# Pairing the 64x64 products of a triangular inverse across four heads, with a new order of the whole program

## The chip, the cores and the metric

The program runs on one core of one Trainium2 chip. The metric is the device time of one execution in microseconds, taken as the median of several runs; lower is better. Five engines work side by side and meet through semaphores: TensorE (PE, with its weight loads shown apart as PEld), VectorE (DVE), ScalarE (ACT), GpSimd (POOL) and SyncE (SP), which here only issues transfers.

## The reference, cut to what matters

One decoder layer on a 1024 x 1024 input: an input projection, two groups of heads (a gated linear recurrence and a gated delta rule), an output projection, and a squared-ReLU MLP. The change lies in the delta rule. Each of its four heads cuts the sequence into chunks and solves a unit lower triangular system in each:

```
Lmat = jnp.where(strict, jnp.einsum('bhnid,bhnjd->bhnij', k_beta, k) * decay, 0.0)
tmat = Lmat + jnp.eye(C, dtype=jnp.float32)
u = lax.linalg.triangular_solve(tmat, v_beta, left_side=True, lower=True, unit_diagonal=True)
w = lax.linalg.triangular_solve(tmat, k_beta * jnp.exp(g)[..., None], ...)
```

The kernel takes chunks of 128 rows, so that there are 8 chunks a head and 32 triangular matrices of 128 x 128. It inverts them once and multiplies by the inverse.

## The kernel before, in words

**Stages.** The start brings in the input `x`, normalizes it, computes a scale `A1` from `w_mod` (`scale0`, `scale1`) and multiplies with the weights of the key projection as they land (`wk0` to `wk3`, each 512 KB; `wk0` comes in two halves). Then come the projections of keys, z, queries, values and the recurrent group, the delta rule among them (`key`, `inverse`, `query`, `value`, `chain`), the output projection, and the MLP: an up stage and a down stage, each of them a seven-product scheme of the Strassen kind. Large products split an operand into a high and a low part (`xh` by an ACT cast, `xl` by a DVE subtraction) and take three matmuls (`mm3`).

**The down stage.** It computes seven products, numbered `at` = 1, 2, 6, 5, 7, 3, 4 (line 1648), each over eight steps `d`. A step needs a left operand `L{d}_{at}` and a right one `R{d}_{at}`, each loaded from DRAM as 512 KB into one slot and split into two more slots (`L..h`, `L..l`); for `at` 5 and 7 POOL first subtracts a second loaded block from the right operand. 24 matmuls use a pair. The last products go to the banks `dn13` and `dn4b`, half a bank each, and DVE, ACT and POOL turn them into the last rows of the output (`final_parts`, line 1561).

**The inverse.** `inverse` (line 956) first inverts all 32 x 32 diagonal blocks, then fills in the off-diagonal parts: `it` and `iy` with 32 x 32 products for two groups of two heads, then `iw` and `iz` with 64 x 64 products for each head. Per head, `iw(h)` is one product a chunk from the lower to the upper half of the partitions, `after_iw` (ACT, line 1020) scales it into `AW`, and `iz(h)` takes that back from the upper to the lower half; `after_iz` (DVE) copies it into `LT`, which `chain` reads. The two kinds of product use different quarters of the PE array. `mms` (line 442) records a list of matmuls as one entry; every head's `iw` or `iz` is two entries of four products (`q0` = 0, 4). `mixed` (line 1026) puts two lists into one entry, in turn. Before the change, heads are handled in pairs (0, 1) and (2, 3): `iw` of the first alone, `iw` of the second mixed with `iz` of the first, `iz` of the second alone (lines 1040 to 1050).

**The order.** Nothing runs in the order of the code. A `Recorder` (line 240) takes every operation with its dependences; `emit` (line 306) issues them by a written-out list `ORDER`, unpacked from the literal `_ORDER` (line 115). Each engine, and each queue of transfers, works through its own part of that list strictly in order, and waits for what an entry depends on. `SLOTS` (line 217) says which of the 46 and 6 slots of 512 KB in the on-chip memory, or of the 8 PSUM banks, a tile gets; a tile can be written only when the last reader of the slot's tile before is done. Most operations pass through one helper, so the profile puts them on L319, those of `mms` on L445; tiles are known by name.

Of the kernel before, what the change touches and what calls it, by code (L numbers as in the profile page):

```python
# [106 lines left out]
def dram_box(ap):  # L107
# [12 lines left out]
    'I^tDH6_Iq&R(DZ0x`y4mou80mv`ebeR_RE3uZ+yY-Dv+uXD*5MxiQ9Bvz1mzb$m;cXu2#hcAO}zH4n7v(fxE2{iCepjl|MYxe2SO!MgvqO*VRl24K&<D1pvl'  # L120
    'EuLLj5&pt7f+nA%Z$!s!<6BF9o@$I_SbZ4@*n5{{t<*-Zpq1lE$uJm!FL^nG`aOX!nGDIx7tDi!SZ*fsGQN`wn6I7P<>yk53e#Nl&u_=_Y>#vkgP#m}Q-;wT'
    'tmtw3WVs1YBi@T$bfGUHx!1_8HVJ!5lije6!}wkRe+yG3*$1t(gr%I72C&&yauls+OG{Y*ZLXl!@*C{4C9Q>)?w4(}QB<@0qyX%>Jr$O<*j)ozO<Adtd<D5Q'
    'hLt42Dn`Jjs$w-)rMql_b{^mzrYk)_6LD`KX3v2q@8J6T;12F5ea#qe6xLe+vbh2|K5xA!mYpoeKwcMd_p-ekkL#TDn(t?W;79S0PJj;5RPGjRMn6h#*h7l+'
    '#_IFaD%mb-TiLMx47nk{N;7x{W1b1nZvncO{*?N7eulD39QQCEQ!2e~CXw1-8qG3?vG)ob1A9rLhh!ywrcgTlW`c4L$H`pjhQ14=E#06^<{)O8>-`!GU`;n9'
    'JFF>aXNt#+yCjeIQt*3Rb&_ke1T9soKf}K3&=$FA+hv0$u2Mm%$}yPX8hpI0nNM43G%Rd9?=?5!V{ENQe{Q00$P(P=4;dii=s`}G{aF7I!*l_wJZO?lX^ywP'
    'x7+NZ!Mxoh$Xx1(H7u0+yvsa5Ur>r1G1a*-tv08;4Z*EIfmnak3P76B44ZJ(nR;0)DnkeGEsM9<EHFVz<_^KZJX`jf80@Sd=b$&ZzxkGyQWeT)ddp<056c2l'
    'V!Z(w&r4(>tklpf>||rq#Pn=(otjZjpiVBVI+kAJQ6_;}+gTgR<iN;`R?w^>c2Sy44@-cz(a2y{=$`3A`We6HNlPvbTMfY9bC8(zR1afAl5`*Bo0ap>VRMG^'
# [1596 lines left out]
```

## Time and profile before

| | us |
|---|---|
| median of 3 runs | 1123.45 |
| lowest and highest run | 1123.28, 1124.21 |
| span of the profiled execution | 1121.3 |
| PE busy in the span | 1111.5 |
| DVE, ACT, POOL busy in the span | 795.0, 622.0, 254.0 |

The profile shows one execution, from its first to its last instruction; what the runs add around the span is 2.15 us. No time of its own is given for the profiled execution beside the span, so a change of the span is added to the median. Matmuls overlap: the record of a 512-column matmul lasts about 395 ns, while the next one starts after about 232 ns, so what a matmul costs is read from the starts of two neighbours.

### The profile page before, as it was taken

What the parts mean: (1) busy time and instruction counts of PE and PEld (TensorE: products, weight loads), DVE (VectorE), ACT (ScalarE), POOL (GpSimd) and SP (SyncE); (2) the same over time, 40 slices, a digit from 0 to 9 for tenths busy, and PEclk for the clock granted to TensorE, in tenths of its full rate; (3) what the DMA queues carried; (4) which work ended last, traced back from release to release, by engine and by line L of the source; (5) the groups of instructions that cost most, each with busy time, mean ns of one, the idle gap of its engine ahead of it and who ended that gap; (6) DMA issues with size and microseconds to landing.
All of it is one profiled execution on the core that took longest, in us unless ns stands there. A gap on an engine that the chain in (4) does not pass through costs nothing.

```text
span 1121.3 us, 16537 instructions
## 1 busy us (share of the span) xinstructions
PE 1111.5 (99%) x6282; PEld 934.3 (83%) x6282; DVE 795.0 (71%) x1122; ACT 622.0 (55%) x967; POOL 254.0 (23%) x159
## 2 busy tenths in 40 slices
PE   9999999999999999999999999999999999999997
PEld 8889889999988877888888888788888888888886
DVE  4859886877878796888675767768664583874573
ACT  6549644466488973786555545556555333453352
POOL 1000100101011442100113123132400366903030
PEclk9999999999999999999999999999999999999999
DMA  9808716567632354321777586778999757954511
GB/s 348 257 20 293 252 38 184 162 195 244 209 96 95 114 206 128 135 85 58 262 239 285 189 277 234 257 243 310 401 397 396 257 183 256 335 173 179 206 75 75
DMA packets 127688, 234.00 MB, mean 209 GB/s; under 512 B 10933, under 2 KB 51450, under 8 KB 127610
## 3 DMA queue, kind: packets, MB, share of 16 engines
q1 hardware_dynamic: 127370, 232.73, 59.8%
q8 instruction: 49, 0.80, 0.3%
q10 hardware_dynamic: 240, 0.23, 0.1%
q14 instruction: 29, 0.24, 0.1%
HBM read 174.18 MB, written 58.74 MB: 208 GB/s over the span
## 4 chain that ended last, share of the span: by engine, by line
PE 93%; ACT 2%; DVE 1%; DMA 1%; issue 1%; SPq 1%; POOL 0%; POOLq 0%; ACTq 0%; DVEq 0%
PE dn L319 27%; PE upx L319 16%; PE upz L319 8%; PE q_p L319 4%; PE k_p L319 4%; PE v_p L319 4%; PE wg L319 4%; PE upy L319 4%; PE ly_p L319 4%; PE lx_p L319 4%; PE wl L319 3%; PE z_p L319 3%; PE ch L319 2%; PE cho L319 1%; DMA wk<-in_w_in_dram 1%
## 5 line engine op out<-in xcount | busy, mean ns | idle before, releaser
L319 PE MATMUL upx<-h2h,U 128*128 128x512 f32 x512 | 167.9, 395 | 0.0
L319 PEld LDWEIGHTS upx<-h2h,U 128*128 128x128 f32 x512 | 96.2, 188 | 22.5
L319 ACT ACTIVATE act<-act 128x512 f32<-128x512 f32 x112 | 70.8, 632 | 58.6 <-DVE act L319 56.5
L319 PE MATMUL upx<-h2l,U 128*128 128x512 f32 x256 | 101.1, 395 | 0.0
L319 POOL TENSOR_TENSOR wd<-wd,wd 128x512 f32<-128x512 f32 x32 | 46.4, 1452 | 236.2 <-DMA wd<-in_w_down_dram 143.5
L319 DVE TENSOR_TENSOR U<-wu,U 128x512 fp32r<-128x512 f32 x112 | 84.4, 776 | 20.7 <-ACT U L319 19.7
L319 PE MATMUL upz<-h2h,U 128*128 128x512 f32 x256 | 85.0, 394 | 0.0
L319 ACT CAST U<-wu 128x512 fp32r<-128x512 f32 x112 | 65.4, 617 | 19.9 <-DVE wu L319 18.2
L319 PEld LDWEIGHTS upx<-h2l,U 128*128 128x128 f32 x256 | 48.1, 188 | 11.8 <-issue 0.4
L319 PEld LDWEIGHTS upz<-h2h,U 128*128 128x128 f32 x256 | 48.1, 188 | 11.1
L319 ACT COPY ek<-upx 128x512 f32<-128x512 f32 x48 | 28.0, 583 | 51.3 <-PE upx L319 50.8
L319 PE MATMUL upz<-h2l,U 128*128 128x512 f32 x128 | 50.3, 393 | 0.0
L319 DVE TENSOR_TENSOR act<-upz,ek 128x512 f32<-128x512 f32 x32 | 22.1, 690 | 36.7 <-ACT ek L319 17.9
L319 POOL TENSOR_TENSOR R<-R,R_5o 128x1024 f32<-128x1024 f32 x8 | 24.5, 3077 | 80.6 <-DMA L<-aod 69.9
L319 PE MATMUL upy<-h2h,U 128*128 128x512 f32 x128 | 42.7, 395 | 0.0
L319 DVE TENSOR_TENSOR wu<-wu,wu 128x512 f32<-128x512 f32 x48 | 36.0, 760 | 2.1 <-DMA wu<-in_w_up_dram 1.9
L319 ACT ACT_TABLE_LOAD x24 | 30.8, 1283 | 2.5 <-issue 2.1
L319 POOL TENSOR_TENSOR ssq<-ssq,mhalf 128x1 f32<-128x1 f32 x16 | 12.8, 805 | 81.1 <-DVE ssq L319 81.0
L319 PE MATMUL q_p<-hh,q_wh 128*128 128x256 f32 (+2 forms) x96 | 30.1, 339 | 0.0
L319 PE MATMUL v_p<-hh,v_wh 128*128 128x256 f32 (+2 forms) x96 | 29.8, 340 | 0.0
L319 PE MATMUL q_p<-hl,q_wh 128*128 128x512 f32 (+2 forms) x96 | 29.7, 336 | 0.0
L319 PE MATMUL lx_p<-hh,lx_wh 128*128 128x256 f32 (+2 forms) x96 | 29.6, 333 | 0.0
(576 smaller groups left out, 3468.4 us busy)
## 6 DMA issues: line engine op xcount, KB each, us to landing
L<-aod SPq DMA_DIRECT2D x56, 512.0 KB, 5.1
R<-in_w_down_dram SPq DMA_DIRECT2D x40, 512.0 KB, 7.2
wu<-in_w_up_dram SPq DMA_DIRECT2D x32, 512.0 KB, 4.5
aod<-as SPq DMA_DIRECT2D x64, 256.0 KB, 5.6
wd<-in_w_down_dram SPq DMA_DIRECT2D x32, 512.0 KB, 5.2
aod<-act SPq DMA_DIRECT2D x48, 256.0 KB, 2.7
x<-in_x_dram SPq DMA_DIRECT2D x16, 512.0 KB, 3.6
sc_w<-in_w_mod_dram SPq DMA_DIRECT2D x16, 512.0 KB, 7.9
```

The costliest lines, as they stand in the source:

```text
L319: op.fn(*[res(v) for v in op.a], **{n: res(v) for n, v in op.k.items()})
```

## The change

`inverse` now steps over the heads: `iw(0)` alone, then `iw(h)` mixed with `iz(h - 1)` for h = 1, 2, 3, then `iz(3)` alone. The products are the same 64; they stand in 10 entries instead of 12. `iw(2)` and `iz(1)`, which stood alone, now share two entries.

```
-        for g in (0, 2):
+        for h in range(NH + 1):
             for q0 in (0, 4):
-                mms(iw(g, q0))
-            after_iw(g)
-            for q0 in (0, 4):
-                mms(mixed(iw(g + 1, q0), iz(g, q0)))
-            after_iz(g)
-            after_iw(g + 1)
-            for q0 in (0, 4):
-                mms(iz(g + 1, q0))
-            after_iz(g + 1)
+                mms(mixed(iw(h, q0), iz(h - 1, q0)) if 0 < h < NH else iz(h - 1, q0) if h else iw(h, q0))
+            if h:
+                after_iz(h - 1)
+            if h < NH:
+                after_iw(h)
```

Both literals are replaced as well, and that reaches the whole program. Unpacked (base85, zlib, running sums), the old list has 8199 entries and the new one 8197. Read engine by engine, with the recorded operations beside them:

| | old list | new list |
|---|---|---|
| PE entries | 5469 | 5467 |
| PE entries that keep their order (longest common run in order) | | 2493 |
| DVE, ACT, SP entries that keep their order | | 797 of 1122, 668 of 914, 356 of 543 |
| slots with the same number | | 90 of 1572 |
| stretches of `iw`, `iz` and second `iy` on PE, with full-size matmuls between stretches | iw0; iw1+iz0; iz1 then iy1; iw2; iw3+iz2; iz3 | iw0 then iy1 then iw1+iz0; iw2+iz1; iw3+iz2; iz3 |
| full-size PE entries from iw2 to the next stretch, and from there to iz3 | 7, 7 | 4, 4 |
| stretches of the start's small products (`sc1_r`) | 2 | 4 |
| before the first matmul that needs the second half of `wk0`: transposes of `x`, key matmuls | 17, 7 | 20, 10 |
| first 13 transfers on SP | | the same |
| PE in the down stage: share of entries that follow their neighbour in the code | 0.95 | 0.01 |
| down stage: fewest matmuls from the last read of a slot by PE to the first matmul on an operand loaded into it | 145 | 28, 36, 42, 43, 47 |
| down stage: the same for an operand part split into a slot | 50 | 8, 8, 9, 9, 12 |
| entries on `dn4b` after the last one on `dn13`, at the end | 24 | 16 |

The 28 belongs to `R5_6` (`at` 6, loaded from a stored sum of `w_down` blocks). The four tightest split parts are `R4_6l`, `R6_2l`, `L0_5l` and `R3_4l`, all made by a DVE subtraction. In the new list of DVE, at the end, the order is: the scaling of `dn13` (`t`), its addition to `xb`, the last pass for `fin6`, that for `fin7`, and then the scaling of `dn4b`.

More of the change, by code (lines that the diff above doesn't have):

```diff
@@ L120 @@
[L120 to L127, printed above, removed]
@@ new lines @@
+    'f;IH>s2V{kOQ}<NqPeDXTRH?~3vF3s+R<wJLwhboEWwXAb`(awdE?UOv?)<Zc<wr!)HHP3M&k*MF`Bq!6#^rJlreJ;yuqTA$aFvRj+WT5T(1!c}?YVg8TNymE}sdE^6'
+    'qUQX%`y-iZ}PPwiTj;53S9LpzdWtD!e)#MtVChC1sME2=AO_kzm=R~BAoYr)5DYSb{)5|ULmb|KO>lJ-kCdgpDphNhd82vuAFf&MyRPWX1G+C}_C(hZX%jvb3mglnzq'
+    'j&P5R*`3AyspqPSoRMcFOBqJ`dO+E$pWp-cU!as=dWbOrDeU|K?{FqR9=#oXyXCdphd8>ldFupGktxoz2sXhDrS*U`k?%zx6<nE(nM7TXf8RW**Nz_ox$9)%boHo7C5'
+    'VU<gzAmwbJra=3zfn^2<>@r!8f+Hj$E=-NpU$Ar?r)Zl$EKWYsyL-KehRSb51#%ZdE0(JwSbI>-=xnO45!y9@MulAdeHVp_xh?mM507Ek(W8Q!^UJ}!WNu4@*s^{kB0'
@@ new lines @@
+    '0rIAv)pz*xrgo7T`Y$<wy{~9)#-9#Pf6X|ZG-9L+bhkbw1^GTv&gp#32tFcmQB}Pz(IbpMt88bE)uSs@heRJpy<dK2>^Z?(5%-7B&y442GiI8Ht1`Q&ob|KtX9wBAHA'
+    'VUEb!|mYMFaMx=qPzk%gI>q(pW#2J2h2H^ZjN0p0PCs<&&hWEY<sEkbdV^Fu%2WUbksIIig!NKj*au^~bcUj*%+ZV;881$`iCuOLBp>wOU4JgX;)>y}(R<z>0}-nDI1'
+    'X)JJJ&yVjA<^bz^f8`9q+j{eXF%;qd-C(=%D{?y-yl@(Z_dU#zZ2XrBpyGrlMTwla;@8}Wfg55J><xy%^p4BAzNbC7`lCoSeyeD$x3U-{$yF_pwk;nLyB(vpyy>wHg*'
+    'VdlIM@Np`8a<qv0P?=od?4?8SJ!uyVVV%4`v{giL{ycKjf|upGrz>RD!IabwrtjYx*yMftZihfwv)%{b7&aTnn*T1E7`z$DgP`uXz3>T#T;2r6qSuQ=@mPy7vvVkQ%B'
@@ new lines @@
+    'cEBdJxf>{fli?ewFGf(Pj95>_-WC@bx;a2BcQF6zIurB0R>IvxM+)soEhcdg7{Mrjphv>b*g8R9eg*DS|s0k>R7$Pa!Ap12IU8p`LAgl{IvGg$R2Sn;wH!#*V?Me0Vf'
+    '%W%I)pV4vB4C`FhOj5xu_L-%jo9Qi*X89+aVhKZk=D>Ryq_O+P&-Gq1>Nt1Am*Lpv|Kiv+eDf5qTmL!|l^1oe`xZOz@NM{<!}aus7+X5tP4+W&qATdf^8K^=F|m_Cge'
+    '>A%J>m_P&|xl%zbMJ_6Qj;4h5ZtD9weX9iT>ZNobHxe^=FyuKbH3Tsa)}fi&RaCOws53IBB5cBfVo&iRU$b0v1h_bwuK2jdAs2cg`=CvA(@)=X1$kSJWGpY~~4!Vwqc'
+    '|ANu`Zs)Qtov2e-gVqd`b0uO6lg8WIYQQZVq4{25SFjXtT0e|XMea}yjh49fi-WQdUKBN0a+V~XNDH-$(?L4g$B%dyDRq*y{O@<3DXog^?Y`jko&mRH>PTujqF`9LfA'
@@ new lines @@
+    'KxX)ammT+3He@M(d8}+ky6<ob6fR<UegM)(6@A_bb)W?#^Sr2QXsM;HX`EPAJ^*12a$TQLGqX@<A+E+_pKlACW8J5b3919&&zOK;a}FHjCZ<!SaRuMIPhu4^@cnckd_'
+    '|w>~%Z!0e@GdJ9)~uaKB!J|Ic%ML+P)BWuE>_<mbjW#mGEc^(3DjB|BF38zqHN&ms%GB9C!wIlS3MKf!hh(!n*8F21<i<P-5(Icdjyzm()?-qc-kyDoM)<X7KB7U0z;'
+    'ZjIh0XM7X=9M;;eJN;Gtlzh@r?~YE3`GCz!n%6nl@_jeM=a3riNB=c_G^D3<dd)w9b>~W5{Y;+J7n#{vvP(l^L3NsDa&yV5xuiO|X)MuLm+{Wmz3|(EV7D8-{lw+MH_'
+    '6O6E3Z-hB2r&k$d|DskdRxlNW;iOz7gLRmMQLWpCkv#%qOH85t}04xQF~?S3r(}g$pq9Ys@rJ?r=q7qhy=k6`33>Bu&6Y41CPek93psjC?4$+hhG2vWRw@y3c$Dy#Aa'
@@ new lines @@
+    'kt=$;+Lo!pV;A=z5&yj(#&rmB(VO&QXI5`$s8FMnu#lTDi2E7jEXTn|EK<!aotS#V<nD*5kl7p<2DDD2@<fmN{-((iMGMQM(%A9|JN%r9R^sv4ujoV}wty-q@K{*Xey'
+    'L!DZDM_wkG$IFMm1QnE;Rt;GldI!@*R$>k|AW?t@5<r7rf!+P8xL7Vze-zMb%oUTrhTlP^F&~xBxpl-g=3aiufR@cQEH{={U<$uRd#AOX-w8h2XY*vy@K^}an31O>VJ'
+    '{@xT-5UE1Um+DZu}~Uqv$*2C`v|IWmxUNsKT(BQu0d0#~MOev@=qaDe=W(dCzMob?)hcv<&oHg_xEO@cYM^V$JxXG&8y3E1<Rc9&LUnw5cxuF)cFCDmg2BmH!iv?SKf'
+    'Xm&jndst3HpY-Y7A>yYC2<@-N9o4bMIz^F62ed#3+8U*Aqg6fyanF%uPHJHhcgh><lyn)%jEg|%i+EuRM^16>72hAuoi2NI9NOSGV{0F5m>j7j1LT6w;vUj5v~>oRvJ'
@@ new lines @@
+    'Zv2N~fZPKLIC?n$H;XRj^i4-X}WWp}p61IOmk$y`#^}^pwgtPtop6j4KsuMcq|xh)PuaJ5BD^rQ)<yY@nMJ*_i5ro=*h@pSXP3@k!YYFmpz7W6Nc+_3j?O%AJshY4=D'
+    'hgXD~y0`;pS7xg)Mw#=1)B1w-XT21Ti^aG+i9e#_-zhq!+g)8r~qH^j)j-Y+sl;5uJi6kX-ixrElayeXrZj#cvMyl#c^xn_0TIBLIv6b#_Z=7MXG|sVir4#o1OQ~12L'
+    'Sz&;$Yjb6uHGo+^+!g38Qr{vexsawnM39Lx@d*e9j+6{MuLjY;;AK`*5dl2I}5TaVYkur`MEBEd(UfL5U$$Q=HiC?dTw`WR;j32qRx$i2NuUBM>5HWGSqh`r=Yp<uG5'
+    'v+s9NL-db+P<(iJfmlymWfJ=Z^tl-AQQ_9@B1_sihYpJM$u*2tZb)iRm>he&Q1a8>M{$Ux}^3T~HowSyXa&eDVEnC@<ie@`+Ioy_0u*VoA<ow)K4SLK0cHic^FsJ;pE'
@@ new lines @@
+    'Cc`CL{maDSYEY5_7NRiHX|)`92Qw;|+BQ1REkx_o)Gu8NpB(Lb^+G}=a8%hBc6gn9I+VPW7j!rfyibzh+8(Z-I@-u8{p1b!u$mOn9Wd<{ZR}Is2|Tch7UoJbn0Bq!)+'
+    '=bBSLH4KdPq-sA1#rD2F^k?kca9bLF#&|cDA@{`UMK4u%2hG$wc;CU)6Qu^^`n{60X8IJ*n3ANM7`Oe=3gGu+>57qxq-<dTSeZ8*x`yTES^c$QI)mRX?J&4C9PY0nL}'
+    '@<ed)0^H^qbJM%eAi)A<?v)kui<NZcdMH%(69PSl4Amy}<Tj|fZqS}V|>mmE(6F&lbc0#Y@WQ3N9uIn2d>kTgAwNGzXhf(K{E@0uPDG0H1j*<V)(&KeriDQ1VQ0IQEO'
+    '=3+V2SDJfj5v>@vX#E@^6i{6lv$<fYsBYB7<?!--@Vu@3o+b|`gF2CM`bmJto@p_A%8^VJ?$s$WQp$e&NU@U&vEsqocEMVkrBST>xOFg+MAYh={D3yNA&U%bk!i3EPb'
@@ new lines @@
+    'T0-l18s`e4v{7S!YjEL%_R@ZY(bel;2MUKCz+JxRRnAb+i;ofH&%7D*Q>fT$+vJeN*t>RLBb2ZMuRWQT%8-92D^YEYq_sFIWYDVIoIE{+!W@XuDw7JDJxsB2$EdiW91'
+    ')YuECkh+nvqSt3dx=?$ZhpX!m0c*hLelko^VtNBC>)@WJbhDJzU*K@BrkSELnlq}%z52X9>DFpZtXvelE`%R4Nb4|$pQTW2apYgvG^0F0|63%TE8#Ct9puoi?qht|pZ'
+    'cyp(X|!JyhWBxqW42Oh}J)ZQMUL$qF=`Pf~fQ$ayIB%6pP5-Xk$OzZKR4mgYxV~e3gN@s>mjN$9Hu#h`h__=w$hif87;^u@j}7H1S8%a#?OhHj4Ofs{`E5*eaCgyC}U'
+    '8zMread{)Ba7qP-*TIx$K8{@~hrua5L<J{+?jLFFf$)mm8t<v(^$aI7KpQydpTvqAD70J?E?(!#Pxcpn+mq9+}j{BIt!Q9SMJB^m7V?$kzV3{YhG!{QEUu#!?+FkMKr'
@@ new lines @@
+    'MrK}Wsns2wx0B_%6iWEnhcjs<2WDSo`Ey(p~k98wegT-CSPrXP5Yn$dQ%1U!D3xBk4wcqx4U;!r$nbPvfO&ejiHXqEe+&OxkM(rO70uN-%&VhE3uzXzR)GH42fA{rBO'
+    'zQHBn7lY^J*QygLUQWvAN6sn18A)SCX7<a7!Cgu6r}Ci#6Xqh6EUdY^yKwFN0NWfU1Efe6f{!<lCnvfv!)uCJ5B@qw;G=MP6cYyjO>^JGUSMdV&zDB8nU!)~W-HHujJ'
+    'guWZ-=vezGG2sWg!qooWZ^f^*$cu^wJS*S32Jr5BW_`Q#XU;{U*K`D}iVk$8KyL;3>I8B1m`-Az9YAz5;ySZ@#T8FW%+G?GzCb@;ffegZm)H#Vr5H<Z@zbQbpW*nSYL'
+    'B?9{!hj@8jd`UhO1!6=GqHnukmghwwd8K_*5C`vZG!;^8G=@F>0I2;QcFVsZWW~@3j!>`m8o0YR#9u$?B)|u#WTBB~h=7p>Z!NB`f-NRBC}}#!z|XAdlxG-XHMk18P5'
@@ new lines @@
+    'Vo&7NCowvP5?RP@mw9$!S&8wS_1cc1P^2@a+^IL@GJ%^9a=o{##CTeR#<54)(rF^tv>;f6@NMzadzVcec#ZHCQwres(YN113C5m#$J=A73V|PY>O>G&a7S&!l)ioy5e'
+    'u!4hga_`2_lnSS7uc&aUd*l&+`q{viSmx?#P~e<`wG?Mb~RmI9Zbw~^>mRGgWq<#a=uK0lMUB5x*~kKjWd21)7`h}JR<K2^3!iR2n%f>imNcTO}Y`k)z^a5z;C0%8p?'
+    'd%$n}OLvPo|Eu!8;u?`6S;<)o3{O!kP%xAKBa!RP6vl2nCNMo}j$paS?34$3GcK>2u=nM&HpJ@Ti&sLQAy6VMpfWtu()Cr)!u;~iUbMC0mwcfTf3jXffJiRL|cKTB9u'
+    'vz5xBZj8T`IDDGexu#jP7}@w^vg2NkZPx{irG+NDkF=*8_dBs&I?3;n{VlQ|uiX>r6sq1we2o9MxPoMn#bEXt**2Mcl_F)q+#KR^tY0Suh-QyxP1ih!wo0Hr*`UvmBg'
@@ new lines @@
+    '?yNG6COB)bcW)G4}-r8990hel6yTh7~3(uE|=>9jA^wO~qE0tgxFojF+~t*3s#)((oI#JXc&6Q|J?8DUq5oEA~KSIu@#m6;~0lS9Gon)5V-+>lCSeA_}n!HqD7nPSt1'
+    'pda+zul^XqS`4lx+8TC3}8^L`qOB+AcfhM?c4(HU787LwrW5{nidHseAHXY06^Dhy32buddsw5@Cn(^(CklD|L)sa+qNU>)R`lye-dYK;n(Dn5Fl6*$BkxoYYbU~$BR'
+    'J`E!QhBd~0Xu0@$e#`2)j!D{iHu<?_0wM7-!HS_n5>+0j-DMgcw0A;h>3>v*5{~bHoFdf6!U&6@`D^pEgVe{Tm5oU8$ZR@$unV-qKw>Buj+L7sMk=**{ZaoLLTX@e#$'
+    '_ODJGwT!QAk8KC)>Mu>K(G>@YF#uoMRu^W8-vuqs%5UcQ6xKhS}GNTg>hDnAhe+2mKLLrzXb-<$<46V<AZ6sZ|zIRH(Ofm*et-|gnhL*%pT=mJ|OUq)OW;nO5}o=7R='
@@ L227 @@
-    '_W5^*hvyFBHec)&>sR{oiY0u1*ugiusM;wxQ+>AIs;`{8<m3H&Yx2+aR*v8gkGS-$OVi^zCsw?4F8};wKRs-lhF;QV!XsuI^ABzo;ktGAyvZqal7093==O2b'
-    '5pA|YPrvJ9cJJ;q{K|_Qt)okplz!+p&dkeeepz7c@1L8u`JWh9X-)32&raw)wumk~?k1K-xos_Q9g?ZZQ)?;5JswJC_uw1oj~{yO%}_pm_iJoN<`V8l4&m_G'
-    'j2X#x>qF2(p4|6OM*KG6<8n~vPxh~4mr=stMh5$~x{vE_?pDQKVE6YX&)D{vj;BwyJax?f2U-ukVE'
+    'c-lQwiL!$>43rPqoB@&tIS62IxFH1c|NmB{)2SG+uq|n|UI6%+0R9^oa?f`i6@<xOddZ&EJ&y7+dolnGnhadQJ<Sy$cz`U>T4^|e{}3l&;rYg{sgl>5KyDoUcVS7J`j'
+    '8e~)7N&KjfAnxBPo~^TFZ#f9LU$8e)Ssypx{3f|30;W|E)=BPHBPy5>RoNI%EQvB;<oH*qs&-K^Vnq0g}m>#jDJD$u&pRTxhPVx|gs58?s74!`U=D0ENcYx)Lg`oN7$'
@@ L230 @@
+    'yd-nD3}asTa1-B0Fs@f+rp|Bg`!U2;?5fay`BLx~gDK3uCC4@e+buWC<$A8_sD*L=UJHL6E{|=t(2K$}rP986ePayw>vXusanRrPABW^_dH'
 )
```

174 lines of the change are left out of this document (73 added, 101 removed).

## The prediction

> **What bounds the kernel now.** The page comes first: its busy times and the chain of work that ended last.
>
> ```profile
> PE 1111.5 (99%) x6282; PEld 934.3 (83%) x6282; DVE 795.0 (71%) x1122; ACT 622.0 (55%) x967; POOL 254.0 (23%) x159
> ...
> PE 93%; ACT 2%; DVE 1%; DMA 1%; issue 1%; SPq 1%; POOL 0%; POOLq 0%; ACTq 0%; DVEq 0%
> ```
>
> PE is busy for 1111.5 of 1121.3 us and makes up 93% of the chain. So there are two ways to a shorter time: fewer or cheaper PE instructions, and less of the 9.8 us in which PE is idle. The view of what PE waits for splits the second. Two of its rows touch a place where the new list differs from the old one:
>
> ```profile
> PE k_p L319 <- ACT wkh L319: 0.7, 1, 0.7
> PE sc_r L445 <- DMA sc_w<-in_w_mod_dram: 0.6, 1, 0.6
> ```
>
> The rest of PE's idle time is the way in (the first weights have to land) and the way out after its last matmul. In the last stage, which the new list shuffles most, PE has no idle time to give. The busy time of PE in a stretch of 100 us shows it (columns: stretch, sum, mean per core and instructions, granted clock, DMA share, GB/s), and so does one row of the chain:
>
> ```profile
> 900.00:1000.00 100.00, 100.00 (x433) 1.00 0.70 244
> ```
>
> ```profile
> 802.48 306.44 PE dn L319 x1320
> ```
>
> PE is full, its granted clock is 1.00, and a 512-column matmul costs 306.44 / 1320 = 0.232 us from start to start. Whatever the new order does there can only be neutral or a loss.
>
> **The inverse: one group and two stretches fewer.** Rows of the chain around the old stretches, then PE's instructions around the mixed one of heads 0 and 1:
>
> ```profile
> 171.81 0.67 PE qk L319 x6
> ...
> 174.95 1.14 PE iy L445 x96
> ...
> 181.80 1.07 PE iw L445 x16
> ```
>
> ```profile
> 166.50 0.28 PE L319 MATMUL v_p<-hl,v_wh 128*128 128x256 f32 x1
> 166.62 0.28 PE L319 MATMUL v_p<-hh,v_wl 128*128 128x256 f32 x1
> ...
> 170.01 0.40 PE L319 MATMUL q_p<-hh,q_wh 128*128 128x512 f32 x1
> ...
> 170.34 0.27 PE L445 MATMUL iw<-aw,LT 64*64 64x64 f32 x1
> 170.35 0.27 PE L445 MATMUL iz<-LT,aw 64*64 64x64 f32 x1
> ...
> 171.42 0.39 PE L319 MATMUL q_p<-hl,q_wh 128*128 128x256 f32 x1
> 171.65 0.50 PE L319 MATMUL qk<-q0T,kTl 128*128 128x128 f32 x3
> ```
>
> A lone group (two entries, 16 records) costs 1.07 us. The mixed one, with twice the records, runs from 170.34 to 171.42, which is 1.08 us: an `iw` and an `iz` start 0.01 us apart, so the second is free. The change makes three mixed groups and two lone ones of two mixed and four lone: six groups become five, **-1.07 us**.
>
> Around a stretch something is lost twice. The 512-column matmul ahead of it takes 170.34 - 170.01 = 0.33 us in place of 0.23, and the 256-column one behind it 171.65 - 171.42 = 0.23 in place of 166.62 - 166.50 = 0.12, together 0.21 us. Six stretches become four: -0.42. Inside the stretches the kind of product changes once more than before (`iw`, `iy`, mixed, in place of `iz`, `iy`); the rows show no price for that, the nearest is one of the two changes above, so 0 to 0.1, and I take the dearer: +0.10. Sum **-1.39 us**.
>
> In exchange the heads become one sequence: a mixed group cannot begin before ACT has scaled the `iw` ahead of it.
>
> ```profile
> 182.91 0.60 ACT L319 ACTIVATE aw<-iw 64x512 f32<-64x512 f32 x1 [0.80 <-PE iw L445]
> ```
>
> The group that began at 181.80 ended at 182.87; ACT started 0.04 us later and took 0.60. With 0.1 for the way back to PE that is 0.74 us. The second `iy` (1.14 us) covers it behind `iw` 0. Behind `iw` 2, and again behind `iw` 3, stand only four full-size entries instead of seven: three or four of 512 columns, the rest of 128 or 256, 0.80 to 0.92 us. That covers 0.74, so I cost these waits at nothing; if ACT is in the middle of another 0.60 us instruction, each is up to 0.5 late. In-order queues put nothing else at stake: behind the waiting PE entry the whole of PE stands, which is the same 0.5.
>
> **The start.** The old gate is the second half of `wk0`:
>
> ```profile
> 17.59 0.62 ACT L319 CAST wkh<-wk 128x512 fp32r<-128x512 f32 x1 [2.38 <-DMA wk<-in_w_in_dram]
> ```
>
> ACT idles 2.38 us until the transfer lands, casts, and PE resumes 0.7 late, the first of the two waits above. The first 13 transfers are the same in both lists, so the gate stays where it is. The new list puts 3 more transposes (0.67 / 6 = 0.11 each) and 3 more key matmuls (0.12) ahead of it, 0.69 us: so the wait is filled. But it also breaks the small `sc1_r` products into four stretches in place of two, and by the price above two more cost 0.42. So between -0.7 (the extra stretches fall ahead of the gate too) and 0 (one falls on a transfer of `sc_w`, which has a wait of 0.6 now); I take **-0.3**.
>
> **The tail.** The list of DVE at the end:
>
> ```profile
> 1111.78 0.42 DVE L319 TENSOR_TENSOR t<-dn,g_bc 128x256 f32<-128x256 f32 x1 [0.41 <-PE dn L319]
> 1112.13 0.74 DVE L319 SCALAR_TENSOR_TENSOR fin<-xb,ssq,fnw 128x512 f32<-128x512 f32 x1
> 1112.78 0.42 DVE L319 TENSOR_TENSOR xb<-xb,t 128x256 f32<-128x256 f32 x1
> 1113.24 0.43 DVE L319 TENSOR_TENSOR fin<-xb,fnw 128x256 f32<-128x256 f32 x1
> 1113.78 0.16 DVE L319 SCALAR_TENSOR_TENSOR sq<-ssq,sq 128x1 f32<-128x1 f32 x1
> 1114.62 0.42 DVE L319 TENSOR_TENSOR t<-dn4b,g_bc 128x256 f32<-128x256 f32 x1 [0.69 <-PE dn4b L319]
> ```
>
> Before, PE takes 1114.62 - 1111.78 = 2.84 us for the 24 matmuls between `dn13` and the last of `dn4b`, 0.118 each, and DVE is done with the four operations in between after 2.00 us (1113.78). After, 16 matmuls leave 1.89 us for the same four: DVE is 0.11 late and PE is no longer the last. Bounds: 0, if they get closer together, to 0.3, if the order of `fin6` behind `xb` exposes ACT or POOL; **+0.1**.
>
> **The down stage.** 306 us whose order is entirely new. The price is in the re-use of slots. Before, at least 145 matmuls (33.7 us) lie between the last read of a slot and the first matmul on what is loaded into it; now the shortest are 28 (`R5_6`), 36, 42, 43 and 47: 6.5, 8.4, 9.7, 10.0 and 10.9 us. In that time SP must issue, the transfer land and ACT cast. For split parts at least 50 matmuls (11.6 us) become 8, 8, 9, 9 and 12: 1.86, 1.86, 2.09, 2.09 and 2.78 us for one DVE subtraction. The rows of the steps, first issues (median us to landing), then the tile `R` (ns, least/median/most):
>
> ```profile
> L<-aod SPq DMA_DIRECT2D x56, 512.0 KB, 5.1
> ...
> R<-bdd SPq DMA_DIRECT2D x16, 512.0 KB, 10.5
> ```
>
> ```profile
> L319 SPq DMA_DIRECT2D R<-bdd x16: 359/368/462, 845.3 to 1054.6; - x16
> ...
> L319 POOL TENSOR_TENSOR R<-R,R_5o x8: 2408/3266/3391, 870.1 to 954.6; 128x1024 f32<-128x1024 f32 x8
> L319 ACT CAST R_5h<-R x8: 1034/1050/1053, 876.7 to 958.5; 128x1024 fp32r<-128x1024 f32 x8
> L319 DVE TENSOR_TENSOR R_5l<-R,R_5h x8: 1214/2748/3430, 880.7 to 964.7; 128x1024 fp32r<-128x1024 f32 x8
> ...
> L319 DVE TENSOR_TENSOR R_4l<-R,R_4h x8: 1218/1224/1714, 1048.2 to 1087.7; 128x1024 fp32r<-128x1024 f32 x8
> ```
>
> A raw loop costs 0.37 (issue) + landing + 1.05 (cast) + 0.1. With 5.1 for the landing that is 6.6, and `R5_6` with its 6.5 is just late; with 10.5 it is 12.0, and `R5_6` is 5.5 late, the next up to 3.6, though a stall of one also gives the others time. The 10.5 was measured on loads issued far ahead, many of them in flight at once; a load that SP issues only when its slot comes free stands in a shorter queue, so I take it nearer to 5.1. While SP waits for that slot, the loads behind it on its one queue wait too. A split loop costs the subtraction + 0.1: 1.32 with the usual 1.22, which fits 1.86 and 2.09; 3.53 with the longest, 1.67 late for the loops of 8 and 1.44 for those of 9. Below nothing is excluded, since PE has no wait here. From 0 to 6.2 or so; I take **+1.0**: `R5_6` half a microsecond late, and as much over all the others.
>
> **The sum.** -1.39 - 0.3 + 0.1 + 1.0 = -0.6 us, counted on the span (1121.3 to 1120.7). What the runs add around the span is taken to stay, so the median goes from 1123.45 to **1122.9 us**. Without the down stage it would be 1121.9. About 0.2%, or 2.25 us, is what a measurement of this kernel can tell from no change, so all this is "the same".
>
> **The rivals.**
> (A) Faster: both waits of the start vanish with no price for the stretches (-0.7 - 0.6), and the down stage and tail cost nothing: -1.39 - 1.3 = -2.7, 1120.8. For it: both waits are in the profile, and the new list fills the first entirely. Against it: two more stretches, and nine tight loops that must all hold. Chance 0.15.
>
> (B) Slower: DVE's subtractions in the tight split loops run beside POOL's. The profile shows the stretch: `R_5l` is made while POOL subtracts, and its median is 2.75 us, against 1.22 for `R_4l`, where POOL is quiet. At the long end the loops of 8 are 1.67 late and those of 9 1.44: two 3.3, three 4.8, four 6.2. With three, 1123.45 - 1.39 - 0.3 + 0.1 + 4.8 = **1126.7**; with four 1128.1. It decides from 3.8 us of lateness in all (1125.7). The long landing of `R5_6` (5.5, so 1127.4) ends in the same place. Against it: POOL has only 16 such subtractions in 306 us, and the four tight parts belong to products that need none themselves. Chance 0.27.
> The Trainium skill, page "SBUF — State Buffer", section "Who interferes with whom", says that a VectorE instruction with two SBUF inputs contends with a GpSimd instruction that reads SBUF, and that the one that comes second is blocked entirely. The trace agrees: the 1.22 us become up to 3.43, which is about one POOL subtraction of 2.41 more. By that rule each tight split that meets POOL is late in full, and (B) has no half measures.
>
> (C) The change doesn't do what it says: in the new mixed group the records of `iz` cost their own time beside those of `iw`, and only the stretches are saved: -0.42 + 0.10 - 0.3 + 0.1 + 1.0 = +0.5, **1123.9**. Against it stands the mixed group, 32 records in 1.08 us. Chance 0.03.
> The Trainium skill, page "TensorEngine Tiling (Array Packing)", section "Instruction Overhead", states about 60 cycles of overhead for each matmul whatever its columns, by which pairing would save nothing. Here the trace decides against it for products on different quarters.
>
> **How the numbers follow.** The forecast, with (C) and all that lies within 0.2% (1121.2 to 1125.7), has 0.58; (A) 0.15 faster; (B) with the long landing 0.27 slower. The forecast's own range is 1121.2 to 1125.7. For 8 in 10 the range runs from 1120.6, just below (A), to 1128.0, which leaves out four late splits or a late load besides late splits: about 0.07 below and 0.12 above.
>
> **What would show it.** Right: four stretches of `iw`, `iz` with 32 records in the middle ones, 1.08 us each; no wait of PE for `aw`; the wait for `wkh` gone; PE's busy time 1 us shorter; `t` on `dn4b` starting without idle time. The view of PE's waits then lists `dn` for the first time: for `R5_6` behind ACT's cast, about 0.5, and for split parts behind DVE, if at all. Wrong: waits of `dn` for DVE of 1.4 us and more with POOL's subtractions beside them (B); mixed groups of 2 us (C); or a wait in a stage that I took for untouched, since the list is new everywhere.

## The result and the profile after

The changed kernel takes 1150.77 us in the median of 4 runs (1148.53 to 1154.36), the kernel before 1123.47 on the same chip: 1.0244 times as long (95% interval in brackets, here and below: [1.0228, 1.026]). The forecast was 1122.9, and the upper end of its range, 1128.0, lies 22.8 us below the result. The profiled execution, the slowest of the four, took 1154.36 us with a span of 1152.6, 31.3 more than the 1121.3 of before; the median lost 27.3.

The page of the new kernel, its busy times and the engines of its chain (which could be followed back over its last part only):

```profile
PE 1122.8 (97%) x6282; PEld 936.2 (81%) x6282; DVE 784.3 (68%) x1122; ACT 623.5 (54%) x967; POOL 247.2 (21%) x159
...
PE 16%; DVE 1%; issue 1%; ACT 0%; POOLq 0%; POOL 0%; DVEq 0%; ACTq 0%
```

PE has the same 6282 instructions. It is idle for 1152.6 - 1122.8 = 29.8 us in place of 9.8, and busy for 11.3 us more. The view of what PE waits for (total, times, longest) now has many causes, all small:

```profile
PE dn L327 <- DVE L_6l L327: 5.3, 3, 2.9
PE dn L327 <- DVE L_5l L327: 3.7, 1, 3.7
PE upx L327 <- ACT ek L327: 1.9, 2, 1.7
PE rows_ps L327 <- DMA rows<-in_lru_conv_w_dram: 1.9, 1, 1.9
PE dn L327 <- ACT R_7h L327: 1.8, 1, 1.8
PE h2T L327 <- ACT h2r L327: 1.3, 2, 0.8
...
PE ch L327 <- DVE q_dm L327: 1.1, 1, 1.1
PE z_p L327 <- DVE LT L327: 0.9, 1, 0.9
```

In the down stage, DVE's subtractions are late beside POOL's. The timeline from 906 us on, first DVE's, then POOL's and PE's (start, duration, engine, work; in brackets the idle time ahead of it):

```profile
906.29 1.22 DVE L327 TENSOR_TENSOR R_6l<-R,R_6h 128x1024 fp32r<-128x1024 f32 x1
907.42 3.43 DVE L327 TENSOR_TENSOR L_6l<-L,L_6h 128x1024 fp32r<-128x1024 f32 x1
```

```profile
906.96 2.82 POOL L327 TENSOR_TENSOR R<-R,R_5o 128x1024 f32<-128x1024 f32 x1 [20.98 <-DMA R_5o<-in_w_down_dram]
```

```profile
911.00 0.47 PE L327 MATMUL dn<-R_6h,L_6l 128*128 128x512 f32 x1 [1.30 <-DVE L_6l L327]
```

The first subtraction began before POOL's and takes 1.22. The second begins 0.46 us into POOL's and takes 3.43; PE takes up its result 0.15 later, after 1.30 us of idle time. The rule that the prediction cited from the Trainium skill ("SBUF — State Buffer", "Who interferes with whom"), that the second is blocked until the first is done, would end it at 906.96 + 2.82 + 1.22 = 911.00; the trace has 910.85.

The longest wait for an `L_6l`, 2.94 us, comes later and indirectly. That subtraction itself takes 1.21 us, but it stands in DVE's list behind two that POOL had stretched to 3.42 and 3.24 (from 930.18 on; POOL subtracts from 930.08 to 935.86) and behind one that sat idle for 1.12 us until ACT's cast of its operand:

```profile
930.18 3.42 DVE L327 TENSOR_TENSOR L_6l<-L,L_6h 128x1024 fp32r<-128x1024 f32 x1
...
942.07 1.21 DVE L327 TENSOR_TENSOR L_6l<-L,L_6h 128x1024 fp32r<-128x1024 f32 x1
```

A longer wait is paid twice. PE's timeline after that one:

```profile
943.34 0.50 PE L327 MATMUL dn<-R_6h,L_6l 128*128 128x512 f32 x1 [2.94 <-DVE L_6l L327]
...
946.19 0.63 PE L327 MATMUL dn<-R_6h,L_6l 128*128 128x512 f32 x1
946.62 0.63 PE L327 MATMUL dn<-R_6h,L_6h 128*128 128x512 f32 x1
...
948.49 0.39 PE L327 MATMUL dn<-R_6l,L_6h 128*128 128x512 f32 x1
```

Matmuls of the same shape start 0.43 us apart for a while, in place of the usual 0.23. PE's windows (stretch, sum, busy and instructions, granted clock, DMA share, GB/s) show both losses: the 100 us that were full before hold 376 matmuls in place of 433, with a mean clock of 0.97, and in the worst 15 us the clock is 0.89.

```profile
900.00:1000.00 100.00, 91.00 (x376) 0.97 0.67 230
935.00:950.00 15.00, 12.06 (x46) 0.89 0.32 106
```

**Where the 31.3 us went.** Worked out from the starts of all matmuls in the two traces (a gap is a distance to the matmul ahead that is more than 0.25 us over the usual one):

| part | before to after, us | change |
|---|---|---|
| start, first 22 us | gaps 1.3 to 0.3, but smaller distances take most of it back | -0.1 |
| 64x64 products | 6.44 to 5.38 | -1.1 |
| gaps from there to the down stage | 1.4 to 13.4 (16 gaps) | +12.0 |
| rest of that part, in smaller distances | not taken apart | +3.5 |
| gaps in the down stage | 0 to 12.0 (6 gaps) | +12.0 |
| down stage, distances of 0.28 to 0.48 us in place of 0.23 (32; 21 of them 427 ns, 6 the first behind a gap) | 0 to 5.2 | +5.2 |
| from PE's end to the end of the span | 6.75 to 6.65 | -0.1 |

The first `dn` comes at 813.4 us in place of 802.3; with the 3.25 us of the 14 up-stage matmuls that now stand inside the down stage, 813.43 - 802.32 + 3.25 = 14.4 us are lost ahead of that stage, and the +3.5 is what the other rows leave of them. PE's end moved from 1114.59 to 1145.92, so the down stage lost 31.33 - 14.36 = 17.0; its two rows sum to 17.2, so its other distances give 0.2 back. (The 13.9 us in an expectation below counts only 12 of the 14 matmuls.)

### The profile page after: what moved, and what is told of

Same layout as the page of the kernel before. It is cut to its first block, busy times and chain, and to the rows that moved or that the text cites. A ratio compares the mean times of both kernels' runs of the same rounds, so it can differ in the third digit from the quotient of the medians.

```text
span 1152.6 us, 16526 instructions
## 1 busy us (share of the span) xinstructions
PE 1122.8 (97%) x6282; PEld 936.2 (81%) x6282; DVE 784.3 (68%) x1122; ACT 623.5 (54%) x967; POOL 247.2 (21%) x159
## 5 line engine op out<-in xcount | busy, mean ns | idle before, releaser
L327 PE MATMUL v_p<-hh,v_wl 128*128 128x512 f32 (+2 forms) x96 | 29.5, 337 | 0.0
L327 PE MATMUL dn<-R_6h,L_6l 128*128 128x512 f32 x64 | 24.2, 412 | 5.3 <-DVE L_6l L327 5.3
L327 PE MATMUL q_p<-hl,q_wh 128*128 128x258 f32 (+2 forms) x96 | 29.4, 335 | 0.0
L327 PE MATMUL v_p<-hl,v_wh 128*128 128x512 f32 (+2 forms) x96 | 29.4, 338 | 0.0
```

Source lines behind the costliest of these rows:

```text
L327: op.fn(*[res(v) for v in op.a], **{n: res(v) for n, v in op.k.items()})
```

## The experiments

The theory from the two traces: the pairing is harmless; the loss belongs to the new order, ahead of the down stage and in it, since producers now deliver just in time. The rivals: the pairing itself costs; one single late operand starts a chain of waits; or the clock, not the waits, is at the root. Each expectation says what its theories were at that time.

### The pairing alone

`pair_old` keeps the order of before and only moves `iz(1)` into the stretch of `iw(2)`. On DVE that takes the copy behind it along:

```
-COPY LT<-iz
 SCALAR_TENSOR_TENSOR g_acc<-g_w,cact,g_acc
...
 COPY S<-ch
+COPY LT<-iz
```

> The old list, with only the inverse regrouped: the stretch of iw2 also takes iz1, and the scaling of iz1 back into LT moves behind it on DVE; all else in the old order. Theory (the order of the new list costs the time, the pairing saves): one group and one stretch fewer, 1.07 + 0.21 us, so 1122.2 us, and no wait of PE on aw. Rival (the sequence of heads makes PE wait for ACT's scaling and delays what is queued behind it): 1125 us or more, with a wait on aw in the view of PE's waits.

1126.38 us (1125.9 to 1127.23, 11 runs) against 1123.57: 1.0023 [1.0014, 1.0032]. No wait for `aw` is there. But PE arrives 1 us earlier at operands whose producers did not move, and a copy that was moved stands ahead of one that is urgent; inside the new mixed stretch the first `iz` now waits for ACT to release its bank. The waits that the kernel before does not have:

```profile
PE lrus_r L445 <- POOL msum L319: 1.0, 1, 1.0
PE ch L319 <- DVE r L319: 0.7, 1, 0.7
PE v_p L319 <- ACT v_wh L319: 0.7, 1, 0.7
...
PE iz L445 <- ACT sq L319: 0.2, 1, 0.2
```

`pair_old2` takes these four away. Besides the lines here, the transposes of `qtok` come two matmuls earlier on PE, and `q_dm` and 33 later buffers get other slots:

```
-COPY LT<-iz
 SCALAR_TENSOR_TENSOR r<-ch,neg_eg,nv
+COPY LT<-iz
...
+CAST v_wh<-v_w
 ACTIVATE v0T<-v0T
...
-CAST v_wh<-v_w
```

> The old list with the inverse regrouped, as in the first experiment, but with its side effects undone: the scaling of iz1 moves behind r on DVE, the last transposes of qtok go two matmuls earlier so that iz1's bank is free, the cast of v_wh goes ahead of the activation of v0T on ACT, and q_dm takes another slot. Theory (the pairing saves what the prediction said, where nothing else is late): the waits for v_wh, r and sq go, 1122.0 to 1122.8 us, 0.7 to 1.4 under the kernel before. Rival (PE's saving only turns into the next wait, since other engines set the pace here): 1123.4 to 1125 us, with a wait for another operand within the next 20 us.

1122.80 (1122.39 to 1125.7) against 1123.63: 0.9999 [0.999, 1.0008]. One wait was left, `cho` for `vn`, 0.7 us at 255 us, because ACT makes `vn` behind an activation on `q_gb`. `pair_old3` moves that activation behind two `vn` and a copy; `pair_old4` moves it the other way, into ACT's idle time ahead of a cast:

```
+ACTIVATE q_gb<-q_gb
 CAST gw<-gwt
-ACTIVATE q_gb<-q_gb
```

> As the second version of the pairing in the old list, and the activation of q3_gb on ACT, which PE's wait for vn stood behind, moved two operations back. Theory (each wait that eats the saving can be moved away one at a time): the wait for vn goes, 1121.9 to 1122.4 us, clear of the kernel before by 1.2 or more. Rival (the saving is eaten again further on): 1122.6 to 1123.5 us.

> As the second version of the pairing in the old list, with the activation of q3_gb on ACT moved ahead of the cast of gw, into idle time of ACT, instead of behind vn. Theory (the saving of the pairing can be kept when the operation that a wait stood behind goes into idle time): the wait for vn goes and no other comes, 1121.8 to 1122.3 us. Rival (other engines' chains set the pace of this stage, and what PE saves is waited for elsewhere): a new wait of 0.5 us or more between 250 and 300 us, 1122.6 to 1124.5 us.

`pair_old3`: 1124.23 against 1123.70, 1.0004 [0.9995, 1.0013]; the wait only moved, to `oT` for `nv`, and became 1.5 us. `pair_old4`: **1122.69** (1122.09 to 1124.89, 11 runs) against 1123.77 (15 runs), 0.999 [0.9981, 0.9999]. Its list of waits is that of the kernel before, which is what 1.1 us less of products needs in order to be seen. Its median is the lowest here, but `pair_old2` lies within the noise of it, and its interval only just leaves 1 out.

### Which half of the new order

`newup_olddown` joins the new order up to the down stage with the old order of that stage; `oldup_newdown` joins the order of `pair_old` with the new down stage. Both had to give some 60 buffers of the down stage other slots.

> The new list for all stages up to the MLP's up stage (pairing included), and the down stage's operations in the old order. Theory (the loss is in two parts that do not depend on each other: 13.9 us of PE's time before the down stage, in some sixteen short waits, and 17.2 us in the down stage): the down stage runs at 0.232 us a matmul with no wait over 0.3 us, and the time is 1134 to 1138 us. Rival (the new down stage is only late because the stages ahead of it hand it over late): the down stage still has waits of several us, time 1145 us or more.

> The old list up to the MLP's up stage (inverse regrouped), and the down stage's operations in the new order. Theory (two independent parts): no waits before the down stage beyond those of the kernel before, the waits on L_6l, L_5l and R_7h in the down stage return with the matmuls at a lower clock behind them, time 1122 + 17 = 1139 us, within 4. Rival (lateness handed over from the stages ahead): 1122 to 1127 us.

1167.15 us, 1.0388 [1.0374, 1.0402], and 1163.41 us, 1.0358 [1.0342, 1.0373]: both are slower than the new kernel. The first time lies where the rival put it (1145 us or more), the second in neither range. The part ahead of the down stage can still be read. The gaps there sum to 10.7 us with the new list, at the same operands as in the new kernel, and to 5.0 with the old one (4.9 in `pair_old`). So the loss upstream belongs to the new upstream list. The down stage was spoilt by the join: its gaps are 26.3 and 28.6 us, first of all these, from each kernel's view of PE's waits:

```profile
PE dn L321 <- ACT L_6h L321: 12.5, 1, 12.5
PE dn L321 <- DVE L_6l L321: 6.6, 1, 6.6
```

```profile
PE dn L331 <- DVE L_6l L331: 11.2, 4, 5.3
PE dn L331 <- DVE L_5l L331: 5.7, 1, 5.7
```

That its slots and the times of its loads come from the list around it may be why an order of this stage cannot be transplanted; no run shows it. How much of the 17.0 us each half carries is not told by these two.

### POOL beside DVE

`no_pool_sub` leaves POOL's 16 subtractions in place with their waits, but makes them short:

```
-            G.tensor_tensor(out=m, in0=m, in1=o, op=ALU.subtract)
+            G.tensor_tensor(out=m[:, :2], in0=m[:, :2], in1=o[:, :2], op=ALU.subtract)
```

> The new kernel, with GpSimd's sixteen subtractions on the right operands of products 5 and 7 cut from 1024 columns to 2 (the rest of these operands stays unsubtracted, so that part of the MLP is not computed). Theory A (DVE's subtractions run long because GpSimd works beside them, as in rival B of the prediction): the splits L_6l and L_5l fall from 3.4 to 1.22 us, at least 9 of the 11.5 us of PE's waits in the down stage and most of the low-clock matmuls go, time 9 to 14 us under the new kernel. Theory B (the list places the splits too late whatever their length, because loads land late): the waits shrink by 2 us each at the most and the time falls by less than 6 us.

1141.82 us (1140.51 to 1142.85), 1.0161 [1.0147, 1.0175]: 9 us less than the new kernel. The gaps of the down stage fall from 12.0 to 2.9 us, the slow matmuls from 5.2 to 0.7, the longest `L_6l` from 3.43 to 1.23. PE's waits for `dn`, all that is left, and the window of the worst 15 us:

```profile
PE dn L334 <- DVE L_5l L334: 1.6, 1, 1.6
...
PE dn L334 <- ACT R_7h L334: 0.7, 1, 0.7
```

```profile
935.00:950.00 15.00, 14.90 (x65) 1.00 0.48 161
```

That could still be the shorter chain from load to cast, and not POOL's company. `pool_scratch` tells them apart: POOL does all its work, but writes it where nobody waits for it.

```
-            G.tensor_tensor(out=m, in0=m, in1=o, op=ALU.subtract)
+            G.tensor_tensor(out=o, in0=m, in1=o, op=ALU.subtract)
```

> The new kernel, with GpSimd's sixteen subtractions as long as before, but into the second operand, which nobody reads (the right operands of products 5 and 7 stay unsubtracted, so that part of the MLP is not computed): GpSimd still works beside DVE, but nothing waits for its result. If it was the company of GpSimd that cost the 9 us which leaving the subtractions out gave back: splits of 3.3 us and waits on L_6l and L_5l return, 1147 us or more. If it was the wait for GpSimd's result that delayed the splits behind it on DVE: about as fast as with the subtractions left out, 1140 to 1144 us.

1149.83 us (1148.38 to 1157.87), 1.0253 [1.022, 1.0285]. The long subtraction is back in the view of the tile `L_6l` (ns, least/median/most), and so are most of the waits: the gaps of the down stage sum to 8.5 us, the slow matmuls to 5.1.

```profile
L334 DVE TENSOR_TENSOR L_6l<-L,L_6h x8: 1214/1220/3436, 882.0 to 939.5; 128x1024 fp32r<-128x1024 f32 x8
```

```profile
PE dn L334 <- DVE L_5l L334: 3.7, 1, 3.7
PE dn L334 <- DVE L_6l L334: 3.1, 1, 3.1
```

So it is POOL's company for the most part. `sub_on_dve` gives the subtraction to DVE, so that POOL subtracts nothing more here and keeps only its other work:

```
-            G.tensor_tensor(out=m, in0=m, in1=o, op=ALU.subtract)
+            V.tensor_tensor(out=m, in0=m, in1=o, op=ALU.subtract)
```

> The new kernel, with the sixteen subtractions of the right operands of products 5 and 7 on DVE instead of GpSimd, at the same places of the list. Theory (in the new list these meet the splits that PE waits for, and two engines that share what they read slow each other): the splits run in 1.22 us, the extra 16 x 1.22 us of DVE mostly fit its idle time, PE's waits in the down stage fall from 12 us to under 5 and the low-clock matmuls with them, time 1140 to 1146 us. Rival (DVE is simply too busy there, whoever does the subtraction): the waits stay, 1149 us or more.

1153.71 us, 1.0265 [1.0251, 1.0279]: no gain. DVE's list is in order, and its timeline shows it standing 9.31 us before a subtraction whose first operand has not landed (`R4_5`, issued at 958.97, landed at 963.62), with the splits queued behind:

```profile
963.70 1.51 DVE L334 TENSOR_TENSOR R<-R,R_5o 128x1024 f32<-128x1024 f32 x1 [9.31 <-issue]
...
974.01 1.21 DVE L334 TENSOR_TENSOR L_5l<-L,L_5h 128x1024 fp32r<-128x1024 f32 x1
```

PE waits 10.4 us for that `L_5l`. Nor did DVE run alone: the four subtractions between these two lines take 2.28 us each, beside POOL's multiplications and additions of 128x512. So this run does not test what DVE would do without POOL. `edf_down` tries the order itself: 60 casts and subtractions of ACT and DVE move ahead of others that are due later, the first ones being

```
+CAST L_2h<-L_2
 ...
-CAST L_2h<-L_2
-CAST L_5h<-L_5
-ACTIVATE fin,sq<-xb
+CAST R_6h<-R_6
+CAST L_5h<-L_5
+CAST L_6h<-L_6
 ...
+ACTIVATE fin,sq<-xb
```

> The new kernel, with 60 of the casts and subtractions that split the down stage's operands moved up on ACT's and DVE's lists, past operations that PE needs later, as far as data and slots allow; PE's list, the slots and all else as they were. Theory (PE waits because a part stands behind others, or is made beside GpSimd's subtraction, with under 2 us to spare; the old list left at least 5.9): the waits of the down stage fall from 12 us to under 6 and the matmuls at 427 ns to under ten, time 1139 to 1144 us. Rival (loads land late or the engines are too slow for the order, whatever the order of the splits): the waits stay above 9 us, time 1147 us or more.

1160.71 us, 1.0325 [1.0311, 1.0339], gaps of 18.8 us in the down stage: worse. The parts moved up wait for their own loads, and what they passed is late instead (the first wait is for an `L_5l`, which DVE ends together with this `sq`):

```profile
PE dn L334 <- DVE sq L334: 5.9, 1, 5.9
PE dn L334 <- ACT R_3h L334: 3.3, 1, 3.3
```

### The clock after a wait

`late_split` makes one wait in the kernel before, far from any other: DVE does one subtraction, `L4_4l`, 9 times.

```
+            for _ in range(8 if i == 8016 else 0):
+                op.fn(*[res(v) for v in op.a], **{n: res(v) for n, v in op.k.items()})
```

> The old kernel with one change: the DVE subtraction that makes L4_4l is done nine times instead of once (same result), which makes it 8 x 1.14 = 9.1 us late; its part had 5.87 us to spare before PE read it. So one wait of PE of 3.2 to 3.3 us in a stage that had none. Theory (a part's time to spare is what decides, and a wait over 2 us costs a second time through the clock): about ten matmuls at 427 ns behind the wait, 1.6 to 2.0 us more, 1128.2 to 1128.9 us. Rival (the slow matmuls of the new kernel have another cause): 1126.7 us.

1130.05 us (1129.69 to 1131.22, 5 runs) against 1123.70: 6.35 us more, 1.0057 [1.0045, 1.007]. PE's timeline:

```profile
1092.41 0.40 PE L321 MATMUL dn<-R_4l,L_4h 128*128 128x512 f32 x1
1096.90 0.80 PE L321 MATMUL dn<-R_4h,L_4l 128*128 128x512 f32 x1 [4.09 <-DVE L_4l L321]
1097.50 0.63 PE L321 MATMUL dn<-R_4h,L_4h 128*128 128x512 f32 x1
1097.92 0.63 PE L321 MATMUL dn<-R_4l,L_4h 128*128 128x512 f32 x1
...
1101.34 0.63 PE L321 MATMUL dn<-R_4h,L_4h 128*128 128x512 f32 x1
...
1102.28 0.40 PE L321 MATMUL dn<-R_4h,L_4h 128*128 128x512 f32 x1
```

The pause is 1096.90 - 1092.41 = 4.49 us, 4.26 over the usual (1 us more than expected). The next start comes 0.60 us later, and ten matmuls then start 0.427 us apart, which costs 10 x (0.427 - 0.232) = 1.95. With the distances at both ends of the ten that makes 6.6 of the 6.8 by which the span grew (1128.1 against 1121.3). In all profiled runs here, each pause of 2.5 us or more in the down stage is followed by 7 to 14 distances over 0.28 us, most of them 427 ns (1.5 to 2.9 us in all), unless the next pause came first; one of 2.15 was too, those of 2.00 to 2.13 were not (their first distance alone was long, 0.31 to 0.34). Ahead of the down stage the length alone does not decide: after 3.62 us in `late_pe` the granted clock of the next 7 us was 0.76, after 3.06 us in `rows_early` it stayed 1.00. The Trainium skill, page "TensorE: Matmul & The Clock Gate", section "HAM oscillation — how this bites in real kernels", lets the clock fall only after idle gaps of more than about 3.4 us; by it the wait of 2.94 us would have been paid once. The trace decides against it. The 427 ns are what its section "Wait — 56ns, not 53.3ns?" gives for the halved clock.

`fill_waits` keeps PE's clock up in the new kernel: ahead of the three longest waits it repeats the matmul before, 10, 13 and 7 times.

```
+FILL = {7004: 10, 7288: 13, 7491: 7}
...
+            for _ in range(FILL.get(i, 0)):
+                last.fn(*[res(v) for v in last.a], **{**{n: res(v) for n, v in last.k.items()}, "start": False, "stop": False})
+            last = op if op.eng == "PE" else last
```

> The new kernel, with 10, 13 and 7 repeats of the matmul before them ahead of the three longest waits of PE in the down stage (2.9, 3.7 and 1.8 us); the repeats add to the sums once more, so these parts of the output change. Theory (a wait of PE over about 2 us costs a second time, as the next ten matmuls run at 427 instead of 232 ns): the waits shrink below 1.5 us, no matmuls at 427 ns follow them, and the time falls by 3 to 5 us under the new kernel, though PE has 7 us more of matmuls. Rival (the slow matmuls have another cause, such as power or contention): they stay, and the time is the same or longer.

1150.65 us (1148.09 to 1153.49), 1.024 [1.0223, 1.0257]: the median of the new kernel, where 3 to 5 us less was expected. In the profiled run, the fastest of them, the gaps fell to 3.1 and the slow matmuls to 1.15 us, with 7.0 us of repeated ones added, so 5.9 less should remain (8.9 + 4.05 - 7.0). The two profiled runs do differ by 6.3, but they are the slowest of the one kernel and the fastest of the other, and the medians agree. It shows that the slow matmuls follow the waits, not that filling pays.

### The waits ahead of the down stage

`late_pe` moves 15 PE entries that wait in the new kernel, with what depends on them, 6 to 15 entries later, for example

```
-MATMUL rows_ps<-ident,rows 128x93
 ...
+MATMUL rows_ps<-ident,rows 128x93
```

`rows_early` treats one cause: nine small transfers of `rows` stand on SP behind two larger ones, which now follow them; on DVE, the casts of `wab` move behind two `hl`.

```
-DMA sh_w<-in_w_mod_dram 128x1024
-DMA wab<-in_w_in_dram 128x8x8
 ...
+DMA sh_w<-in_w_mod_dram 128x1024
+DMA wab<-in_w_in_dram 128x8x8
```

> The new kernel, with the fifteen entries of PE before the down stage that waited 0.25 us or more for an operand or a bank moved 6 to 15 entries later in the list, with what depends on them. Theory (each wait is one entry that stands a microsecond or two too early, with ready work right behind it): 8 to 11 of the 13.4 us of PE's gaps before the down stage go, the down stage keeps its own loss, time 1139 to 1144 us. Rival (the chains on the other engines are late, so that the entry behind waits instead): gaps before the down stage of 9 us or more, 1147 us or more.

> The new kernel, with two transfers (the weights wab and the first block of sh_w) moved on SP's list behind the nine small transfers of rows, which its longest early wait of PE is for; these are then issued about 1 us earlier. Theory (each wait ahead of the down stage is one producer that stands too late in its own queue): the wait for rows falls from 1.9 to under 1.0 us and the down stage starts 0.5 to 1.5 us earlier than in the new kernel (813.4). Rival (the queue of transfers is full, and moving two only trades one wait for another): the start of the down stage stays within 0.5 us of 813.4, with a wait for wab or sh_w.

`late_pe`: 1153.59 us, 1.0269 [1.0253, 1.0285]. The gaps ahead of the down stage sum to 13.6 us, as before (13.4), and one more of 1.0 stands at the first `dn`: what PE does later is late for the next engine, and comes back as new waits.

```profile
PE v_p L334 <- DVE neg_eg L334: 3.3, 1, 3.3
...
PE vtok L334 <- DVE S L334: 2.5, 1, 2.5
```

`rows_early`: 1152.40 us, 1.0255 [1.0231, 1.0279]. The wait for `rows` is gone, and this one stands in its place:

```profile
PE xTp L334 <- DVE cols L334: 2.7, 1, 2.7
```

The last two transfers of `rows` are issued 1.7 us earlier (32.24 and 32.60 in place of 33.90 and 34.26). But DVE's list has the casts of `wab` ahead of the copy into `cols`, and the transfer of `wab` is one of the two that were moved back, so DVE now waits for it:

```profile
DVE wab L334 <- DMA wab<-in_w_in_dram: 2.5, 1, 2.5
```

The down stage begins at 814.3 us (new kernel 813.4): one wait was traded for another, as the rival had it, though the start moved by more than its 0.5 us. No single cause explains the 12 us upstream: there are 16 gaps with a dozen releasers.

## Why the prediction was wrong

**What bounds the kernel.** PE did stay the bound, at 97%. "Whatever the new order does there can only be neutral or a loss" was said of the down stage, but it holds for every stage in which PE is full.

**The inverse.** The group saved is worth 1.06 us against 1.07; no wait for `aw` came. The stretches were mis-sized: the matmuls ahead of them lose 0.55 us in all in six stretches and 0.62 in four, those behind them 0.64 and 0.42, so that of the -0.42 about -0.15 is there. `pair_old4` shows the whole edit in the old order, with a few neighbours moved: -1.1, about the group alone, since it keeps six stretches (`iy1` stands alone in place of `iz1` then `iy1`).

**The start** is -0.1 (predicted -0.3): both waits are filled, and smaller distances take most of it back. **The tail** is -0.1 (predicted +0.1). DVE runs back to back, as predicted:

```profile
1145.54 0.42 DVE L327 TENSOR_TENSOR fin<-xb,fnw 128x256 f32<-128x256 f32 x1
1145.96 0.42 DVE L327 TENSOR_TENSOR t<-dn4b,g_bc 128x256 f32<-128x256 f32 x1
```

**The down stage is the first step that failed**: "From 0 to 6.2 or so; I take +1.0", and it was +17.0 in the profiled run. The loops from the last read of a slot to its next use, by which it was priced, held: `R5_6` was not late, and the parts of the tight split loops came 0.27 to 0.39 us before PE needed them. What was not priced is when DVE's and ACT's lists, as re-ordered, reach a part that has all it needs: behind five of the six gaps DVE began the subtraction the moment it was free, 4.2 to 21 us after the cast that it reads. The lead of a part (from the end of its split to PE's first use, worked out from the traces for all 224) shows how little room was left:

| | before | after |
|---|---|---|
| least lead, us | 5.87 | late |
| parts under 1 us | 0 | 19 |
| parts under 3.5 us | 0 | 57 |
| median, us | 24.7 | 6.6 |

Before, 2.2 us more for a split beside POOL met a least lead of 5.87 and cost nothing. After, 32 parts have less than 2 us. So the mechanism of rival (B) was right (`no_pool_sub`, `pool_scratch`), but at other parts: `L6_6l`, `L2_6l` and `L6_5l` ran 3.29 to 3.43 us, and `L5_6l` stood behind such ones. The sixth gap, 1.8 us, is a loop of slots that was not counted, since its last reader is DVE and not PE. `R4_7h` gets the slot of `L2_7`, and ACT's cast waits until DVE's subtraction from `L2_7`, 3.32 us long, has read it:

```profile
1014.14 1.04 ACT L327 CAST R_7h<-R 128x1024 fp32r<-128x1024 f32 x1 [1.24 <-DVE L_7l L327]
```

And (B) had no price for the clock after a wait, most of another 5.2 us (`late_split`).

**The second step that failed is one that is not in the sum**: the other stages were taken as free, though the text ended on "a wait in a stage that I took for untouched, since the list is new everywhere". They cost 12.0 us in gaps and some 3.5 in smaller distances. An example, of a small gap (0.27 us): `k3T` is made at 110.37 us in place of 106.09, while the matmul that needs it moved from entry 658 of PE's list forward to 644.

**What stays open.** Which order of the producers would free the new upstream list was not found: `late_pe` and `rows_early` only traded waits. Nor does a run show a better order of DVE and ACT in the down stage: `edf_down` made it worse. That waits which the clock may or may not make longer are why four runs of the new kernel scatter by 6 us, and four of the kernel before by 1, is argued and not shown; the mean granted clock of the two slower runs was 0.994, of the two faster ones 0.996, which would be some 2 us. The 3.5 us of smaller distances ahead of the down stage have no cause shown.

## What to carry to other kernels

Judge a re-ordered list by the smallest lead of every operand in every stage, with the durations that its producers have beside each other; totals of busy time do not show it, and loops of slots only where every reader of a slot is counted. A saving on the engine that bounds the kernel makes it arrive earlier at every later operand, so it counts only as far as the producers can follow: the same pairing measured +2.8, -0.8, +0.5 and -1.1 us with four placements of a few neighbours, of which only the first and, just, the last are clear of noise. And price a wait of some 2.5 us or more on PE at about 2 us over its length.

## What the runs showed of the hardware

- After a pause of PE of 2.5 us or more in the down stage, 7 to 14 starts of 512-column matmuls come over 280 ns apart, most of them 427 in place of 232; after one of 2.15 us ten did, after those of 2.00 to 2.13 us none but the first. Ahead of that stage a pause of 3.06 us (`rows_early`) left the granted clock at 1.00.
- A DVE subtraction of 128x1024 takes 1.22 us alone, up to 3.43 beside POOL's, also where nobody reads what POOL writes (`pool_scratch`), and 2.28 beside POOL's additions and multiplications of 128x512 (`sub_on_dve`).
- For a while from 19 us on, SP issued its transfers about 1.3 us apart, whatever their size: until 24 us in the new kernel (512 KB ones of `wk` and the small `wab`), until 31 and 32 us in the kernel before and in `rows_early` (mostly the small ones of `rows`). What sets the 1.3 us is not shown.
